# First stage of a hybrid decoder step planned anew: loads on the sync queue beside the page gathers, TensorE's order pinned, three dense tiles in step

## The chip, the cores and the metric

The kernel runs on one core of a Trainium2 chip. The metric is the time of one execution on the device in microseconds (us); lower is better. The engines are PE (TensorE, matrix products), DVE (VectorE), ACT (ScalarE), POOL (GpSimd) and SP (the sync engine, which only issues DMAs here). Each engine works through its instructions in the order in which they are written to it and waits for the semaphores of others.

## The reference

The program is one step of a single-layer hybrid decoder for 520 tokens: 512 of a prompt and one for each of 8 samples. What matters here is its beginning:

```python
def _layer(x, c, pos, conv_buf, h0, ffn_buf, nsa_fn, p):
    mod = jnp.einsum("bd,de->be", jax.nn.silu(c), p["ada_w"]) + p["ada_b"]
    sh1, sc1, g1, sh2, sc2, g2 = jnp.split(mod[:, None, :], 6, axis=-1)
    h = _rmsnorm(x, p["norm1_w"]) * (1.0 + sc1) + sh1
    proj = h @ p["w_in"]
    z, xbc, dt_raw, q, kv, att_g, merge_g = jnp.split(proj, ...)
    # then: causal conv and SSD scan of xbc, attention with a paged cache, merge, ConvFFN

def _compress(k, pe, w1, w2):      # on the rows of the pages, among others
    part = jnp.einsum("bjshd,sde->bjhe", sub, w1[r * CMP_STRIDE:(r + 1) * CMP_STRIDE])
    return jnp.einsum("bnhe,ed->bnhd", jax.nn.silu(hid + part), w2)

past = cache_nsa_kv[page_table]    # the pages of the samples, gathered by a table
```

## The kernel before, in words

Tokens (520) lie along the free axis and features on the 128 partitions. The function `phase_a` is the first stage. It has five kinds of work:

- **Pages.** 16 gathers (`gather`, an indirect DMA on POOL's queue, 128 x 512 numbers, 262 KB each) bring the pages into the tiles S_13 and KS. `compress_s` multiplies them with the weights w1k and w1v (tile `w1`, four loads of 512 KB). It runs in four parts of 32 rows in the order of instructions (each a fp32 product which the trace shows as two records, so 64 records), each part with four gathers. Afterwards ACT and DVE add the two halves (`ch`, `chs`), and a DMA stores them (`dr_hs`).
- **Modulation.** Eight tiles `ada`, nb = 0 to 7, each with two loads of 512 KB and eight narrow products with the conditioning vector (`sc`, from cT); ACT copies the result to `adas`, TensorE transposes it twice ("flip"), DVE reduces it to `mod`. Tiles nb and nb + 4 together give the shift and scale for the rows h(2 nb) and h(2 nb + 1).
- **Norm.** x comes in four loads of 532 KB. ACT squares it, DVE adds the eight squares, TensorE sums over partitions (`sums`), DVE forms 1/rms (`rstd5`), TensorE spreads it over the partitions (`spread`), and ACT copies it into `rs`.
- **h.** `h(k)`, k = 0 to 7: x times rs, scaling and shift, and a split into a high part `h_hi` (ACT) and a low part `h_lo` (DVE, x minus h_hi).
- **The first dense tiles.** A weight tile (1024 x 128) is split into a high part `wh` (ACT, line 308) and a low part `wl` (line 310, DVE and POOL in turns) in two halves of 512 columns. A dense tile is, for each k, hi x hi, hi x lo and lo x hi on two token halves: 8 x 6 = 48 matmuls. Before, misc and B are computed in step in `phase_a`; C and then the convolution tiles x0 to x3 and z follow outside.

A planner runs through the program once and fixes the order on each engine by its own model of times; an instruction named in `behind` is held behind another in that order without a semaphore. `queue` (line 399) loads on SP, `queue_pool` (line 403) on POOL. Of these, before, SP carries w1, cT and const, then the stores of `dr_hs` and the last modulation weights; POOL carries the gathers, x and the first modulation and w_in weights. PSUM has two wide tiles `d` (dense results, pages) and four narrow ones `s`. A conv tile's result leaves its wide tile through ACT and DVE. `Weights` loads, splits and frees the weight tiles; it has six raw buffers here.

## Time and profile before

| | |
|---|---|
| Median of 3 runs | 1470.51 us (1470.27 to 1474.33) |
| Profiled execution, its own time | 1468.96 us |
| Its span in the trace | 1467.1 us |
| Mean granted TensorE clock | 0.983 |
| PE busy | 1404.2 us (96%) |
| DVE busy | 942.2 us (64%) |
| ACT busy | 697.6 us (48%) |
| POOL busy | 473.7 us (32%) |

The trace has the span of one execution, a little less than its time. Busy times are sums over the span; a stage is read from its own rows.

### The profile page before, as it was taken

The page shows a single profiled execution, that of the slowest core. Times are in us where ns is not written, and L with a number is a line of the kernel's source. Part 1 is how long each engine was busy: PE and PEld are TensorE (multiplying, and loading weights), DVE is VectorE, ACT ScalarE, POOL GpSimd, SP SyncE. Part 2 cuts the span into 40 slices and gives each one's busy share as a digit, 9 for nine tenths or more (in the row PEclk, how much of TensorE's full clock was granted, in tenths as well). Part 3 has the DMA queues.
Part 4 walks back from the last instruction along what each step waited for, and adds up shares of the span by engine and source line. Part 5 has one row for each costly group of instructions (what it writes and reads, how often), then busy time and mean ns, then how long its engine had stood idle before and what let it go on. Part 6 is the DMA issues. An engine that isn't in the chain of part 4 may idle for free.

```text
span 1467.1 us, 28899 instructions
## 1 busy us (share of the span) xinstructions
PE 1404.2 (96%) x11403; PEld 1283.1 (87%) x11403; DVE 942.2 (64%) x1851; ACT 697.6 (48%) x1540; POOL 473.7 (32%) x488
## 2 busy tenths in 40 slices
PE   7899899999999899999999999999999999999996
PEld 6689789998898798887878877899889999999996
DVE  1768899788879856858667562134586636653663
ACT  2346657565664424646556463233554324432443
POOL 6213564463565754312213011122421111111113
PEclk9989999999999999999999999999999999999998
DMA  8734546345354384314122124525423233433221
GB/s 301 296 97 159 176 136 213 112 143 199 122 170 143 117 278 159 110 39 130 59 94 81 44 101 150 182 84 210 164 72 98 82 110 130 137 112 98 80 77 59
DMA packets 73799, 195.30 MB, mean 133 GB/s; under 512 B 8480, under 2 KB 21312, under 8 KB 73408
## 3 DMA queue, kind: packets, MB, share of 16 engines
q1 hardware_dynamic: 67968, 175.05, 36.2%
q0 software_dynamic: 5152, 17.86, 3.4%
q8 instruction: 90, 1.47, 0.4%
q10 hardware_dynamic: 544, 0.54, 0.1%
q14 instruction: 45, 0.37, 0.1%
HBM read 173.10 MB, written 24.49 MB: 135 GB/s over the span
## 4 chain that ended last, share of the span: by engine, by line
PE 69%; DVE 10%; DMA 8%; ACT 4%; issue 4%; POOL 4%; SPq 0%; DVEq 0%; POOLq 0%; ACTq 0%
PE d L385 54%; PE s L385 13%; DMA wr<-w_in 3%; DVE st L417 2%; PE s L1370 2%; DVE S L414 1%; DMA st<-sst 1%; DVE wl L310 1%; DMA P<-pool_kv,idx 1%; DMA csx<-dr_cs 1%; ACT wh L308 1%; ACT E L430 1%; ACT S L430 1%; DVE E L414 1%; POOL wl L310 1%
## 5 line engine op out<-in xcount | busy, mean ns | idle before, releaser
L385 PE MATMUL d<-S,wh 128*128 128x256 f32 (+1 forms) x4640 | 834.9, 291 | 27.2 <-DVE S L414 9.4
L385 PEld LDWEIGHTS d<-S,wh 128*128 128x128 f32 x4640 | 670.8, 191 | 57.7 <-issue 27.3
L385 PE MATMUL d<-S,wl 128*128 128x256 f32 (+1 forms) x2672 | 557.6, 287 | 0.2 <-DVE wl L310 0.2
L385 PEld LDWEIGHTS d<-S,wl 128*128 128x128 f32 x2672 | 423.2, 190 | 5.7 <-issue 4.7
L308 ACT ACTIVATE wh<-wr 128x512 fp32r<-128x512 f32 (+1 forms) x354 | 217.3, 623 | 388.9 <-PE d L385 302.5
L310 POOL TENSOR_TENSOR wl<-wr,wh 128x512 fp32r<-128x512 f32 (+1 forms) x153 | 205.9, 1347 | 607.6 <-ACT wh L308 581.8
L310 DVE TENSOR_TENSOR wl<-wr,wh 128x512 fp32r<-128x512 f32 (+1 forms) x201 | 154.6, 769 | 119.4 <-ACT wh L308 106.0
L385 PE MATMUL d<-M,wh 128*128 128x256 f32 (+1 forms) x960 | 197.0, 284 | 2.4 <-DVE M L417 1.7
L385 PEld LDWEIGHTS d<-M,wh 128*128 128x128 f32 x960 | 149.7, 188 | 3.0 <-DVE M L417 1.9
L430 ACT ACTIVATE P<-s,sm 128x256 f32<-128x256 f32 (+3 forms) x128 | 66.7, 524 | 64.5 <-DVE sm L1352 60.4
L414 DVE TENSOR_TENSOR S<-S,S 128x520 f32<-128x520 f32 (+3 forms) x86 | 65.8, 770 | 31.8 <-ACT S L430 28.7
L1352 DVE TENSOR_REDUCE sm<-s 128x1 f32<-128x512 f32 (+3 forms) x96 | 57.1, 596 | 32.0 <-PE s L385 31.2
L430 ACT ACTIVATE S<-S 128x520 f32<-128x520 f32 (+4 forms) x87 | 49.7, 581 | 49.4 <-DVE S L414 20.8
L417 DVE SCALAR_TENSOR_TENSOR S<-d,fww,S 128x511 f32<-128x511 f32 x84 | 62.9, 749 | 12.0 <-ACT S L430 12.0
L430 ACT ACTIVATE PT<-s 128x512 f32<-128x512 f32 (+2 forms) x96 | 49.9, 523 | 39.9 <-PE s L1370 39.5
L385 PE MATMUL s<-PT,V 128*64 128x128 f32 x640 | 64.3, 286 | 0.0
L417 DVE SCALAR_TENSOR_TENSOR st<-st,dts,so 128x128 f32<-128x128 f32 x128 | 60.0, 517 | 6.4 <-ACT so L430 4.3
L385 PE MATMUL s<-K,Q 128*128 128x256 f32 (+3 forms) x256 | 60.1, 336 | 1.7 <-ACT PT L430 1.6
L422 DVE TENSOR_SCALAR P<-P,sm,gates 128x256 f32<-128x256 f32 (+3 forms) x128 | 58.9, 480 | 2.4
L430 ACT ACTIVATE so<-bcb,xd 128x128 f32<-128x128 f32 x128 | 41.0, 391 | 34.9 <-DVE ys L1060 21.2
L417 DVE SCALAR_TENSOR_TENSOR S<-d,cwh,S 128x511 f32<-128x511 f32 (+2 forms) x72 | 53.4, 742 | 2.4 <-ACT S L430 2.0
L1370 PE MATMUL s<-cst,P 128*128 128x128 f32 x320 | 52.3, 276 | 0.8 <-DVE P L422 0.7
(312 smaller groups left out, 1686.7 us busy)
## 6 DMA issues: line engine op xcount, KB each, us to landing
wr<-w_in SPq DMA_DIRECT2D x75, 512.0 KB, 3.6
wr<-w_up SPq DMA_DIRECT2D x44, 512.0 KB, 3.8
wr<-ada SPq DMA_DIRECT2D x36, 512.0 KB, 4.2
st<-sst SPq DMA_DIRECT2D x32, 256.0 KB, 2.9
csb<-dr_cs SPq DMA_DIRECT2D x16, 512.0 KB, 4.2
o_ssms<-st SPq DMA_DIRECT2D x32, 256.0 KB, 2.1
wr<-w_so SPq DMA_DIRECT2D x16, 512.0 KB, 3.5
wr<-w_dn SPq DMA_DIRECT2D x16, 512.0 KB, 3.4
```

The lines of the kernel that those rows point to most:

```text
L308: self.nc.scalar.activation(hi[:, :n], raw[:, k0:k1], AF.Copy)
L310: eng.tensor_tensor(out=lo[:, :n], in0=raw[:, k0:k1], in1=hi[:, :n], op=ALU.subtract)
L385: r = self.nc.tensor.matmul(out, lhsT=l, rhs=r, start=start, stop=stop)
L414: return (eng or self.nc.vector).tensor_tensor(out=out, in0=a, in1=b, op=op)
L417: return self.nc.vector.scalar_tensor_tensor(out=out, in0=a, scalar=s, in1=b, op0=op0, op1=op1)
L422: return (eng or self.nc.vector).tensor_scalar(out=out, in0=a, scalar1=s1, scalar2=s2, op0=op0, op1=op1)
L430: return self.nc.scalar.activation(out, a, func, scale=scale, **kw)
L1352: nc.vector.tensor_reduce(sm[:, 0], ps, AX.X, ALU.max, negate=True)
L1370: nc.tensor.transpose(ps[:, i * n + k * P:i * n + (k + 1) * P], pr[:, i, k * P:(k + 1) * P], self.ident)
```

## The change

The diff, cut to its core:

```diff
-WARM = 12
+WARM = 10
+FILL = 18
@@ Weights.prepare
-            self.nc.scalar.activation(hi[:, :n], raw[:, k0:k1], AF.Copy)
+            r = self.nc.scalar.activation(hi[:, :n], raw[:, k0:k1], AF.Copy)
+            if self.hold:
+                self.hold(r)
+                self.hold = None
@@ Emit.mm
+        if self.pin is not None:
+            self.behind(r, self.pin)
+            self.pin = None
@@ Emit.dense
+        if apart:
+            d = [self.ps_s()[:, 0:n] for _, _, n in HALVES]
@@ phase_a
+            for i in range(16):
+                g = self.gather(KS[i // 8][:, i % 8].rearrange("p j i c -> p (j i c)"), A["pool_cmp"], i)
+                self.last_pool = self.behind(g, self.last_pool)
+            W = Weights(nc, pa, self.jobs(), self.order and self.order[0], raws=RAW0, parts=PART0,
+                        queue=lambda i: self.queue, first=[first[i // 4][:, i % 4] for i in range(8)])
+            self.queue(cT, A["cT"])
+            W.load(2)
             for j, nm in enumerate(("w1k", "w1v")):
                 for half in range(2):
                     self.queue(w1[:, j, half], A[nm][half])
-                if j == 0:
-                    self.queue(cT, A["cT"])
             self.queue(self.cst[:, :CONST_EARLY], A["const"][:, :CONST_EARLY])
-            def load_x(k):
-                self.queue_pool(x[:, k:k + 2], A["xT"][:, k:k + 2])
...
+            W.load(4)
+            for k in range(0, KD, 2):
+                self.queue(x[:, k:k + 2], A["xT"][:, k:k + 2])
             W.load()
+            self.W.load()
...
             def h(k):
+                self.tt(x[:, k, :], x[:, k, :], r, ALU.mult, nc.gpsimd if k % 2 else nc.vector)
...
+            products(a[0])
+            pin()
+            self.fill(FILL)
+            pages()
+            products(a[4])
+            flips(a[0])
+            pages()
...
+            products(a[1], a[5])
+            flips(a[4])
+            pages()
+            flips(a[1], a[5])
+            pin()
+            self.sums(d, sq, True, True)
+            rb = self.rstd5(d, DM, pa)
+            products(a[2], a[6])
+            self.W.hold = W.hold = lambda r: self.behind(r, self.last_ada)
...
+            flips(a[2], a[6])
+            for k in range(4):
+                h(k)
+            pages()
+            products(a[3], a[7])
+            names = [("C", 0), ("misc", 0), ("B", 0)]
+            tiles = [self.in_tile(n, None if i == 0 else W, i == 0) for i, n in enumerate(names)]
+            for k in range(KD + 1):
+                if k < 2:
+                    h(4 + k)
+                elif k == 2:
+                    flips(a[3], a[7])
+                    h(6)
+                    h(7)
+                for n, g in zip(names, tiles):
+                    try:
+                        next(g)
+                    except StopIteration as e:
+                        self.early[n] = e.value
+            c = self.t(cp, "S2", [P, T], 4)
+            for (_, t0, n), p in zip(HALVES, self.early["C", 0]):
+                self.act(c[:, t0:t0 + n], p)
@@ compress_s
-            nc.sync.dma_start(self.dr_hs[j], hs.rearrange("p x n -> p (x n)"))
+            nc.scalar.dma_start(self.dr_hs[j], hs.rearrange("p x n -> p (x n)"))
```

`pin` holds the next matmul behind the one written before it. `fill` issues bf16 matmuls on a tile of zeros whose result nobody reads. `apart` puts the halves of C's result into two narrow PSUM tiles, from which ACT copies them; `tokens` (not shown) lets the conv tile read either kind of result.

On SP, the head of the program before. w_11 is the tile of w1, cT the conditioning, wr a weight tile, chs the sums of the pages:

```order
L1156 DMA page_88<-page 128x16
L399 DMA w_11_94<-w1k 128x1024 x2
L399 DMA cT_95<-cT 128x256
L399 DMA w_11_94<-w1v 128x1024 x2
L399 DMA cst_63<-const 128x184
L1188 DMA dr_hs_153<-chs_326 128x512
L399 DMA wr_448<-ada 128x1024
L399 DMA wr_496<-ada 128x1024
L1188 DMA dr_hs_153<-chs_332 128x512
```

And the same place of the changed kernel (S_15 and S_16 hold the modulation weights of tiles 0, 4 and 1, 5, S_7 is x):

```order
L1210 DMA page_86<-page 128x16
L408 DMA cT_93<-cT 128x256
L408 DMA S_15_112<-ada 128x1024 x2
L408 DMA w_11_92<-w1k 128x1024 x2
L408 DMA w_11_92<-w1v 128x1024 x2
L408 DMA cst_63<-const 128x184
L408 DMA S_15_112<-ada 128x1024 x2
L408 DMA S_7_85<-xT 128x1040 x4
L408 DMA S_16_113<-ada 128x1024 x4
L408 DMA wr_132<-ada 128x1024
```

The weights of the modulation and x have come to SP's queue, in the order in which TensorE uses them, and the stores of dr_hs have left it; further weights follow without a store between them.

On PE, behind the warm matmuls, before. d_154 and d_155 are the results of the pages, s_351 to s_410 those of modulation tiles 0, 4, 1, 5, and the rows of L595 are flips:

```order
L385 MATMUL d_154<-S_13_102,w_11_94 128x4x4x8 x16
L385 MATMUL d_155<-S_13_102,w_11_94 128x4x4x8 x16
L385 MATMUL d_154<-KS_103,w_11_94 128x4x4x8 x16
L385 MATMUL d_155<-KS_103,w_11_94 128x4x4x8 x16
L385 MATMUL s_252<-ones_64,S_24_253 128x1 x5
L385 MATMUL d_154<-KS_103,w_11_94 128x4x4x8 x16
L385 MATMUL d_155<-KS_103,w_11_94 128x4x4x8 x16
L385 MATMUL s_338<-cst_63,rstdb_291 128x128 x2
L385 MATMUL s_342<-cst_63,rstdb_291 128x128 x2
L385 MATMUL s_342<-cst_63,rstdb_291 128x8
L385 MATMUL s_351<-S_15_124,sc_149 32x256 x8
L385 MATMUL s_360<-S_15_124,sc_149 32x256 x8
```

And of the changed kernel, behind ada0 and the 18 fillers (d_187 and d_188 are the pages, s_221 is ada4, s_293 and s_304 are ada1 and ada5, s_269 the sums):

```order
L391 MATMUL d_187<-S_13_94,w_11_92 128x4x4x8 x16
L391 MATMUL d_188<-S_13_94,w_11_92 128x4x4x8 x16
L391 MATMUL s_221<-S_15_112,sc_151 32x256 x8
L614 MATMUL s_232<-cst_63,adas_165 128x128 x2
L391 MATMUL d_187<-S_13_94,w_11_92 128x4x4x8 x16
L391 MATMUL d_188<-S_13_94,w_11_92 128x4x4x8 x16
L391 MATMUL s_293<-S_16_113,sc_151 32x256 x8
L391 MATMUL s_304<-S_16_113,sc_151 32x256 x8
L614 MATMUL s_315<-cst_63,adas_230 128x128 x2
L391 MATMUL d_187<-KS_95,w_11_92 128x4x4x8 x16
L391 MATMUL d_188<-KS_95,w_11_92 128x4x4x8 x16
L391 MATMUL s_269<-ones_64,S_31_270 128x1 x5
```

The modulation tiles stand between the parts of the pages now instead of behind them; ada2 and ada6 with 12 of the last part's 32 rows follow, then the spread, the other 20 rows, ada3 and ada7, and then the dense tiles.

On POOL, behind the gathers, before (identb and negtri are constants, wl the low halves of weights):

```order
L573 CAST identb_672<-cst_63 128x128
L310 TENSOR_TENSOR wl_1_445<-wr_134,wh_1_444 128x512
L310 TENSOR_TENSOR wl_1_493<-wr_136,wh_1_492 128x512
L575 CAST negtri_674<-cst_63 128x256
L310 TENSOR_TENSOR wl_1_782<-wr_676,wh_1_781 128x512
L310 TENSOR_TENSOR wl_1_851<-wr_678,wh_1_850 128x512
L422 TENSOR_SCALAR gates_760<-gates_760 128x240
```

And of the changed kernel:

```order
L592 CAST identb_760<-cst_63 128x128
L423 TENSOR_TENSOR S_7_85<-S_7_85,rs_155 128x520 x4
L594 CAST negtri_762<-cst_63 128x256
L315 TENSOR_TENSOR wl_1_565<-wr_401,wh_1_564 128x512
L315 TENSOR_TENSOR wl_1_671<-wr_407,wh_1_670 128x512
L315 TENSOR_TENSOR wl_1_659<-wr_144,wh_1_658 128x512
L315 TENSOR_TENSOR wl_1_872<-wr_146,wh_1_871 128x512
```

Four of the eight products x times rs (S_7 with rs) have come to POOL, ahead of all splits of weights; the first two splits of before (misc and B) stood ahead of rs and stand behind it now.

## Rows read from the trace of the kernel before

**Rows 1.** The head of the page: busy times of the engines, and the chain of work that ended last, by engine.

```profile
PE 1404.2 (96%) x11403; PEld 1283.1 (87%) x11403; DVE 942.2 (64%) x1851; ACT 697.6 (48%) x1540; POOL 473.7 (32%) x488
...
PE 69%; DVE 10%; DMA 8%; ACT 4%; issue 4%; POOL 4%; SPq 0%; DVEq 0%; POOLq 0%; ACTq 0%
```

**Rows 2.** The table of stretches of the core: from:to in us, its length, busy us of PE, PEld, DVE, ACT and POOL (with the number of instructions), then the mean granted clock of PE, the busy share of the DMA engines and the GB/s that they moved.

```profile
12.80:47.60 34.80, 34.80 (x308) 33.92 (x308) 8.62 (x17) 7.54 (x14) 20.28 (x31) 0.94 0.93 343
47.60:58.10 10.50, 7.16 (x78) 3.42 (x75) 9.42 (x32) 4.34 (x11) 1.17 (x1) 0.84 0.68 224
58.10:91.85 33.75, 28.25 (x190) 24.78 (x189) 24.29 (x64) 15.04 (x33) 5.29 (x5) 0.80 0.38 142
150.00:250.00 100.00, 92.10 (x722) 84.40 (x721) 92.80 (x163) 67.29 (x172) 56.19 (x59) 0.97 0.54 170
```

**Rows 3.** The timeline of PE from 0 to 100 us: start, busy us, line, operation and tiles, number, and in brackets the idle time before it and what ended it. The rows are, in this order, the warm matmuls, two page parts together and one alone, the sums, the spread, a pair of modulation tiles, a flip, the first dense matmuls behind a wait, C's first with its wait, and six matmuls further of C at full clock, from the start of one row to that of the next, which is x0's first.

```profile
1.39 5.30 PE L385 MATMUL s<-warm 128*128 128x512 bf16 x12 [1.39 <-POOL warm L653]
12.80 16.64 PE L385 MATMUL d<-S,w 128*128 128x128 f32 x128 [6.11 <-DMA S<-pool_cmp,idx]
29.28 7.31 PE L385 MATMUL d<-KS,w 128*128 128x128 f32 x64
36.43 1.17 PE L385 MATMUL s<-ones,S 128*128 128x1 f32 x10
...
44.69 1.18 PE L385 MATMUL s<-cst,rstdb 128*128 128x128 f32 x10
45.80 1.93 PE L385 MATMUL s<-S,sc 128*32 128x256 f32 x32
...
51.99 0.44 PE L595 MATMUL s<-cst,adas 128*128 128x128 f32 x2
...
74.49 0.51 PE L385 MATMUL d<-S,wh 128*128 128x256 f32 x2 [1.68 <-ACT S L430]
...
82.74 1.24 PE L385 MATMUL d<-S,wh 128*128 128x256 f32 x4 [1.66 <-ACT Z L430]
...
91.12 0.64 PE L385 MATMUL d<-S,wh 128*128 128x256 f32 x4
...
91.84 0.64 PE L385 MATMUL d<-S,wh 128*128 128x256 f32 x4
```

**Rows 4.** The DMA of the windows 5 to 7, 7 to 9, 9 to 11 and 35 to 38 us (packets, MB and mean GB/s of the window, for the first and the last; the queue, its packets, MB and the share of the 16 engines' time, for the first three, one row each; q1 is SP's queue, q0 POOL's); the issue of the first gather on POOL (start, us); and the time from issue to landing of the 16 gathers.

```profile
DMA packets 328, 0.81 MB, mean 404 GB/s; under 512 B 35, under 2 KB 163, under 8 KB 328
q1 hardware_dynamic: 328, 0.81, 102.3%
...
q0 software_dynamic: 15, 0.06, 7.5%
...
q0 software_dynamic: 202, 0.69, 84.7%
...
DMA packets 351, 1.27 MB, mean 422 GB/s; under 512 B 42, under 2 KB 42, under 8 KB 351
...
4.34 1.16 POOL L1163 DMA_INDIRECT S<-pool_cmp,idx  x1 [2.35 <-DVE idx L417]
...
DMA to landing us min/median/max: 3.4/3.9/6.2
```

**Rows 5.** The table of stretches, as above, where the granted clock (the number ahead of the DMA share) changes.

```profile
17.00:17.50 0.50, 0.50 (x5) 0.50 (x5) 0.00 (x0) 0.00 (x0) 0.41 (x1) 0.76 1.07 416
...
76.00:88.00 12.00, 10.06 (x46) 9.66 (x46) 6.97 (x21) 3.13 (x6) 0.70 (x1) 0.50 0.00 0
...
89.00:90.00 1.00, 1.00 (x10) 1.00 (x10) 0.01 (x1) 0.99 (x2) 0.00 (x0) 1.00 0.03 0
```

**Rows 6.** The timelines of DVE and, behind the last line of dots, of POOL: the splits of weights (wl<-wr,wh), x times rs (S<-S,rs), scalings (S<-S,a,mod), and subtractions for h_lo (S<-S,S).

```profile
47.80 1.51 DVE L310 TENSOR_TENSOR wl<-wr,wh 128x512 fp32r<-128x512 f32 x1
49.24 4.96 DVE L414 TENSOR_TENSOR S<-S,rs 128x520 f32<-128x520 f32 x8
...
60.56 2.52 DVE L414 TENSOR_TENSOR S<-S,S 128x520 fp32r<-128x520 f32 x4
...
66.45 3.49 DVE L414 TENSOR_TENSOR S<-S,S 128x520 fp32r<-128x520 f32 x2
69.86 0.68 DVE L310 TENSOR_TENSOR wl<-wr,wh 128x512 fp32r<-128x512 f32 x1
...
75.18 0.55 DVE L422 TENSOR_SCALAR S<-S,a,mod 128x512 f32<-128x512 f32 x1 [0.16 <-ACT S L430]
75.64 1.30 DVE L414 TENSOR_TENSOR S<-S,S 128x520 fp32r<-128x520 f32 x2
...
47.51 1.27 POOL L310 TENSOR_TENSOR wl<-wr,wh 128x512 fp32r<-128x512 f32 x1 [0.23 <-ACT wh L308]
...
66.39 2.99 POOL L310 TENSOR_TENSOR wl<-wr,wh 128x512 fp32r<-128x512 f32 x2 [3.05 <-ACT wh L308]
```

**Rows 7.** The timelines of ACT (a table load, the first step of a conv tile, and Z, the copy of misc's result) and, behind the last line of dots, of SP's queue (the first store of dr_hs).

```profile
75.36 1.28 ACT L430 ACT_TABLE_LOAD   x1
...
81.33 0.78 ACT L430 ACTIVATE S<-d,cbh,cwh 128x520 f32<-128x520 f32 x1 [4.45 <-DVE convo L859]
82.01 0.68 ACT L430 ACTIVATE Z<-d,cst 96x520 f32<-96x520 f32 x1
...
47.91 0.33 SPq L1188 DMA_DIRECT2D dr_hs<-chs  x1
```

More of the change, by code (lines that the diff above doesn't have):

```diff
@@ L273, in place, with load @@
         return self.pool, (self.raws if key[0] == "r" else self.parts) - (more or 0)
-    def load(self):
-        while self.loaded < len(self.order):
+    def load(self, upto=None):
+        while self.loaded < (len(self.order) if upto is None else min(upto, len(self.order))):
             i, m = self.loaded, len(self.first)
@@ L499, in dense @@
             for j, (a, b) in enumerate(((0, 0), (0, 1), (1, 0))):
-                for c0, t0, n in HALVES:
-                    m = self.mm(d[:, c0:c0 + n], l[a], r[b][:, t0:t0 + n], start=(k == 0 and j == 0),
+                for out, (c0, t0, n) in zip(o, HALVES):
+                    m = self.mm(out, l[a], r[b][:, t0:t0 + n], start=(k == 0 and j == 0),
                                 stop=(k == nk - 1 and j == 2))
@@ L554, in in_tile, with tokens @@
         w = (W or self.W).get(name)
-        d = yield from self.dense(w, KD, lambda k: self.h_hi[:, k, :], lambda k: self.h_lo[:, k, :], W=W)
+        d = yield from self.dense(w, KD, lambda k: self.h_hi[:, k, :], lambda k: self.h_lo[:, k, :], W=W, apart=apart)
         return d
+    @staticmethod
+    def tokens(d):
+        return d if d.shape[-1] == T else d[:, OFF:OFF + T]
     def setup(self):
@@ L650, in warm, with fill @@
     def warm(self, pool):
-        z = self.t(pool, "warm", [P, 512], dt=BF16)
-        self.nc.gpsimd.memset(z, 0.0)
+        self.z = self.t(pool, "warm", [P, 512], dt=BF16)
+        self.nc.gpsimd.memset(self.z, 0.0)
+        self.fill(WARM)
+    def fill(self, n):
         d = self.ps_s()
-        for _ in range(WARM):
-            self.mm(d, z[:, 0:P], z)
+        for _ in range(n):
+            self.mm(d, self.z[:, 0:P], self.z)
     def phase_a(self):
@@ L694, in phase_a, with pin, products, flips @@
             self.preload(AF.Sqrt)
[L695 to L717 removed]
+            self.h_hi = self.h_lo = None
+            r = self.t(pa, "rs", [P, T])
+            def pin():
+                self.pin = self.last_mm
+            def products(*gens):
+                for g in gens:
+                    for _ in range(3):
+                        pin()
+                        next(g)
+            def flips(*gens):
+                for g in gens:
+                    pin()
+                    next(g)
+                    self.pin = None
+            def pages():
+                pin()
+                next(comp)
             def h(k):
+                self.tt(x[:, k, :], x[:, k, :], r, ALU.mult, nc.gpsimd if k % 2 else nc.vector)
                 a1 = self.t(pa, "a1", [P, 16], 4)
@@ L748, in phase_a @@
-            for n, g in zip(names, tiles):
-                try:
-                    next(g)
-                except StopIteration as e:
-                    self.early[n] = e.value
+            comp = self.compress_s(KS, w1, pa)
+            a = {nb: self.ada(nb, W, pa) for nb in range(8)}
+            products(a[0])
+            pin()
+            self.fill(FILL)
[3 more added lines that the diff above has]
+            pages()
+            d = self.ps_s()
+            sq = self.t(cp, "S2", [P, T], 4)
@@ new lines, in phase_a @@
+            self.behind(self.act(sq, x[:, 0, :], AF.Square), self.last_ada)
+            for k in range(1, KD):
+                s = self.t(cp, "S2", [P, T], 4)
+                self.act(s, x[:, k, :], AF.Square)
+                self.tt(sq, sq, s, ALU.add)
+            products(a[1], a[5])
+            flips(a[4])
+            pages()
+            flips(a[1], a[5])
+            pin()
+            self.sums(d, sq, True, True)
+            rb = self.rstd5(d, DM, pa)
+            self.h_hi = self.t(cp, "S16", [P, KD, T], 4, F32R)
@@ new lines, in phase_a @@
+            self.h_lo = self.t(cp, "S16", [P, KD, T], 4, F32R)
+            products(a[2], a[6])
+            self.W.hold = W.hold = lambda r: self.behind(r, self.last_ada)
+            pin()
+            for part in range(2):
+                lo, hi = self.span(part)
+                cs = self.PARTS[part]
+                self.act(r[:, lo:hi], self.spread(rb[:, cs[0]:cs[-1] + 1], part))
+            flips(a[2], a[6])
[3 more added lines that the diff above has]
+            products(a[3], a[7])
@@ new lines, in phase_a @@
+            for _ in comp:
+                pass
+            pin()
+            names = [("C", 0), ("misc", 0), ("B", 0)]
[9 more added lines that the diff above has]
+                    try:
+                        next(g)
+                    except StopIteration as e:
+                        self.early[n] = e.value
```

82 lines of the change are left out of this document (20 added, 62 removed).

## The prediction

> **What bounds the kernel now.** I read the head of the page first [rows 1]: TensorE is busy in 96% of the span, and it and its two helpers fill the chain that ended last. So a gain can only come from a stretch in which TensorE waits or runs at half clock. The table of stretches [rows 2] shows where that is: from 12.8 to 47.6 us it is busy throughout, but it misses 3.34 us from 47.6 to 58.1 and 5.50 us from 58.1 to 91.85, where the granted clock is also only 0.80, and its timeline shows 7.50 us before the first page part (1.39 and 6.11) [rows 3]. On every engine the order of the two kernels is the same behind the first fifth to quarter of its instructions, so all that the change can do is to shift the instant at which the convolution tiles x0, x1, ... run, and everything behind them, as a block. In the kernel before, x0 starts at 91.84 us [rows 3], right behind the last matmul of C.
>
> TensorE's rows [rows 3] give the prices: a page part (64 records) 7.3 us, a pair of modulation tiles 1.93 us, a flip 0.44 us, the sums 1.17 us, the spread 1.18 us, and six dense matmuls 0.72 us at full clock, so 0.12 us each.
>
> The DMA rows [rows 4] say what can arrive: 404 to 422 GB/s when the engines are full, so about 0.41 MB/us, counted from 3.5 us on. Gathers have 262 KB each.
>
> **The change part by part.**
>
> *Loads on the sync queue.* The order shows ada0 ahead of the w1 tiles, then ada4, x, ada1, ada5. Ahead of the first page part stand 0.13 + 1.05 + 2.10 MB there and four gathers, 1.05 MB: 4.33 MB / 0.41 = 10.6 us, plus 3.5, plus 0.8 to land = 14.9. The ten warm matmuls, ada0 and the 18 fillers (18 x 0.44 = 7.9 us, 0.44 from 5.30 / 12) end at about the same time. I take 15.0, against 12.80 before. What is lost there comes partly back, because ada0 is then done and because before the pages ran at half clock until 17.25 [rows 5].
>
> Pages 1, ada4, a flip, pages 2: 15.0 + 7.3 + 0.97 + 0.44 + 7.3 = 31.0. Then ada1 and ada5 wait for their weights: 8.65 MB on the sync queue (0.13 + 1.05 + 2.10 + 0.09 + 1.05 + 2.13 + 2.10) and all 4.19 MB of gathers make 12.84 MB / 0.41 = 31.3, plus 4.3 = 35.6. At the 343 GB/s that the stretch from 12.8 to 47.6 really moved [rows 2] it is 41.7; that is the other bound. I take 35.6, because the windows in which a queue was full are the nearest rows, and the changed queue has no waits in it.
>
> *TensorE's pinned order.* From 36.1: the rest of ada5 0.35, pages 3 7.3, flips 0.8, sums 1.17, ada2 and ada6 1.93, 12 of 32 matmuls of pages 4 2.7, spread 1.18: 51.5, and the copies of 1/rms (rs) are there at 52.0. Before, rs was there at 49.2 (x times rs starts at 49.24 [rows 6]). So this stage starts 2.8 us later, with more of TensorE's work already done: flips 2 and 6, the rest of pages 4 (4.6) and ada3, ada7 (1.93) are all that stands between rs and the dense tiles, and end at 59.
>
> *From rs to the last h_lo.* This term decides. Before, it took 27.8 us, from 49.15 to 76.94 (its last row starts at 75.64 and takes 1.30 [rows 6]). Four of the eight multiplications x*rs move from VectorE (0.62 us each, 4.96 / 8 [rows 6]) to GpSimd; the rows have none there, but the split of a weight is the same operation on 512 instead of 520 columns: 1.28 us. The bounds are that they run beside VectorE (cost nothing) or in turns with it. The rows point to turns: at 66.45 two subtractions that otherwise take 0.63 us each (2.52 / 4) took 3.49 us while GpSimd ran two splits in 2.99 us, which alone take 2 x 1.28; a split on VectorE at 47.80 took 1.51 instead of 0.68 us while GpSimd's ran from 47.51 to 48.78. So I add up both engines as one: x*rs 4 x 0.62 + 4 x 1.30 = 7.7; remaining reductions of modulation tiles and small operations 4.5; eight scalings 4.4 (0.55 each); eight subtractions 5.0; the two additions behind the pages 1.6; weight splits 4 x 0.68 + 4 x 1.28 = 7.8, of which before one of each was done before rs. Together 31.0, so the last h_lo is ready at 83.0 (before 76.94).
>
> The Trainium skill, page "SBUF — State Buffer", section "SBUF: two separate sides", speaks against moving work to GpSimd for this reason: it has the two engines share one pair of ports under an exclusive lock, so that a VectorE operation with two inputs in SBUF and a GpSimd operation that reads SBUF block one another completely. The trace agrees (3.49 us where 1.26 would do). By that rule the term is 31.0 us, without it 20.7.
>
> *Three tiles in step.* C, misc and B have 3 x 48 = 144 matmuls, 17.3 us. The first low half of a weight is ready at about 69.7: the first 15.8 us of the list above, plus some 2 us in which ScalarE, in program order, puts small copies that wait for VectorE ahead of the weights' high halves. From there 17.3 us give 87.0; the last h_lo gives 83.0 plus two steps of the three tiles (36 matmuls, 4.3 us) = 87.3. TensorE waits from 59 to about 69, and after the wait of 1.68 us before 74.49 the clock stood at half until 89 [rows 3, 5]; here at most a few waiting matmuls meet the low clock, 1.3 us. So the three tiles end at 88.6. Before, misc and B ended at 81.1 (82.74 less C's wait of 1.66) and C at 91.84 [rows 3]. The in-step order gives TensorE 18 instead of 12 matmuls for each step of h (2.2 us against 1.4), so I count no further waits between steps.
>
> *What then waits.* misc and B hold both wide PSUM buffers, so x0 waits for ScalarE: the conv 0.78, a table load 1.28, Z 0.68 [rows 7], 2.75 us together. The kernel before has the same wait for Z ahead of C. x0 starts at 91.35, against 91.84.
>
> *Costless parts.* C's copies out of PSUM (about 0.55 us on ScalarE) lie under x0. The dr_hs stores on ScalarE's queue take 0.33 us of issue [rows 7] in a stage where ScalarE is idle half the time; before, the first of them held the sync queue until 47.91. That wait is gone, which the sum has in it: ada3 and ada7 now wait only for TensorE.
>
> The sum is -0.5 us on the profiled execution's 1468.96: 1468.5. The runs' median lies 1.55 us above that execution, so I forecast 1470.0 for the median.
>
> **Rivals.** A time within 4.4 us (0.3%) can't be told from no change here.
>
> *A, faster.* GpSimd's operations run beside VectorE's. For it: most of VectorE's scalings read only one tile, and not every pair in the trace collides. Against it: the two rows above. The last h_lo is then at 72.7, the first low half at 62.8, the tiles end between 62.8 + 17.3 = 80.1 and 84.5, and x0 starts between 82.9 and 87.3: 4.6 to 9.0 us gained. VectorE is busy 92.8% from 150 to 250 us [rows 2], which may take some back. About 1463. TensorE's work alone forbids more.
>
> *B, slower: gathers behind the sync queue.* From 5 to 7 us the sync queue had all of the engines (102.3%) though a gather had been issued at 4.34; from 7 to 9 the gathers had 7.5%; they moved when the sync queue ran dry, 84.7% from 9 to 11 [rows 4]. Before that cost 3 us at most (landing 3.4 to 6.2). Now the sync queue is full for some 30 us. If the gathers get a share s of 0.41 MB/us, the first four land at 8.3 + 1.05 / (0.41 s) + 0.8: 14.2 at a half, 16.8 at a third, 21.9 at a fifth, 34.7 at a tenth. Each us beyond 15 delays the pages, and all behind them, unless the wait for ada5 hides it: that wait is 5 us long, and the pages' later gathers use it up too. By these terms it decides below a quarter: at a fifth about 1475, at a tenth about 1487.
>
> The Trainium skill, page "DMA: Bandwidth & Descriptors", section "Queues, rings and completion order", has each DMA engine take turns between the queues that have work, packet by packet. By that the gathers would keep a share near a third and B would not happen; the 0% and 7.5% here fit it badly.
>
> *D, slower: the loads come no sooner.* The DMA engines were busy 93% from 12.8 to 47.6 already [rows 2], at 343 GB/s. If the new mix moves no more than that, ada5 is there at 41.7, and rs, h and x0 come up to 6 us later: 1476. Against it: 422 GB/s from 35 to 38 [rows 4].
>
> **How the numbers follow.** My forecast (within 0.3%) 0.41, its own range 1466 to 1474 (1.3 us of clock, 2 us at ScalarE, some overlap on GpSimd). A 0.32. B 0.16, D 0.11: slower 0.27. To leave out no more than 2 in 10, the range reaches from 1462 (A's middle and a little) to 1477 (D, and B down to a fifth).
>
> **What would show it.** The pages' first matmul at 15 to 16.5 us; if it is beyond 20, B. ada5 at 36; at 41 or later, D. Multiplications of 1.3 us on GpSimd with VectorE's operations next to them stretched to about 2 us: the turns; unstretched: A. The last h_lo at 83, x0 at 91.4. The prediction is wrong if x0 starts before 87 or after 96, or if later tiles do not shift with x0.

## The result, and the profile after

The changed kernel takes 1486.72 us (median of 4 runs, 1485.95 to 1487.09) against 1471.0 us of the kernel before (4 runs, 1470.27 to 1474.33) on the same chip: slower by 15.7 us, ratio 1.0102 with the interval 1.0084 to 1.0119. The forecast was 1470.0, with a range from 1462 to 1477. Two executions of later kernels were slow, one of v_adafirst (5431 us) and one of v_adafirst2 (3724 us), and are in no median.

The head of the page after, as [rows 1]: busy time of each engine, and the chain that ended last.

```profile
PE 1411.1 (95%) x11419; PEld 1288.5 (87%) x11419; DVE 948.6 (64%) x1847; ACT 698.4 (47%) x1542; POOL 475.1 (32%) x474
...
PE 73%; DVE 11%; DMA 7%; ACT 3%; issue 3%; POOL 2%; SPq 0%; DVEq 0%; ACTq 0%; POOLq 0%
```

TensorE is busy 6.9 us longer than before with 16 matmuls more; the span grew by 17.1 us (1484.2 against 1467.1). The head doesn't say where. TensorE's timeline does; these rows answer to [rows 3] (start, busy us, line, operation and tiles, number, idle time before it and what ended it).

```profile
8.34 4.06 PE L391 MATMUL s<-warm 128*128 128x512 bf16 x18
...
14.72 7.38 PE L391 MATMUL d<-S,w 128*128 128x128 f32 x64 [2.32 <-DMA S<-pool_cmp,idx]
...
37.50 0.64 PE L391 MATMUL s<-S,sc 128*32 128x256 f32 x8 [0.51 <-DMA S<-ada]
...
68.55 0.80 PE L391 MATMUL d<-S,wl 128*128 128x256 f32 x2 [2.50 <-DVE wl L315]
...
88.62 0.40 PE L391 MATMUL d<-S,wl 128*128 128x256 f32 x2
91.44 0.99 PE L391 MATMUL d<-S,wh 128*128 128x256 f32 x4 [2.43 <-ACT Z L439]
...
109.36 1.21 PE L391 MATMUL d<-S,wh 128*128 128x256 f32 x4 [4.13 <-DVE S L426]
...
143.88 1.02 PE L391 MATMUL s<-xdd,bt 128*128 128x512 f32 x2
```

In order: the 18 fillers, the first page part, the last quarter of ada5, the first low half of a dense weight, the end of the three tiles, x0, x2, and the first matmul of the scan's state (`s<-xdd,bt`). Up to x0 they stand where the forecast put them (14.7 for 15.0, 37.5 for 36.1, 68.6 for 69.7, 89.0 for 88.6, 91.44 for 91.35). x0 starts 0.40 us earlier than in the kernel before. But x2 waits 4.13 us, and the state matmul, which before stood at

```profile
137.78 1.02 PE L385 MATMUL s<-xdd,bt 128*128 128x512 f32 x2
```

comes 6.1 us later. The loss arises behind the point at which I stopped reading, and it grows on the way. Three later rows show where: two further matmuls of the state, and behind them a row of VectorE from which on all engines have the same order again. Before:

```profile
242.25 1.02 PE L385 MATMUL s<-xdd,bt 128*128 128x512 f32 x2
...
293.65 1.02 PE L385 MATMUL s<-xdd,bt 128*128 128x512 f32 x2
...
328.79 1.13 DVE L417 SCALAR_TENSOR_TENSOR st<-st,dts,so 128x128 f32<-128x128 f32 x4
```

After:

```profile
249.14 1.02 PE L391 MATMUL s<-xdd,bt 128*128 128x512 f32 x2
...
307.40 1.02 PE L391 MATMUL s<-xdd,bt 128*128 128x512 f32 x2
...
342.73 1.14 DVE L426 SCALAR_TENSOR_TENSOR st<-st,dts,so 128x128 f32<-128x128 f32 x4
```

The shift is 6.1 us at the first state matmul, then 6.9, 13.8 and 13.9: about 7 us arise in one stretch of the scan, from the first to the third of these rows, which takes 93.6 us instead of 86.5. The last 3.2 of the 17.1 us arise behind it.

Two questions follow: why x0 in time doesn't give the scan in time, and why 6 us become 16.

**From the end of misc and B to the scan.** The table of stretches, columns as in [rows 2], from the end of misc and B to the first state matmul, of the kernel before:

```profile
81.10:91.84 10.74, 9.10 (x53) 9.10 (x54) 8.07 (x23) 4.73 (x8) 1.83 (x2) 0.64 0.01 2
91.84:118.30 26.46, 26.46 (x215) 25.30 (x214) 18.44 (x41) 18.12 (x42) 4.43 (x6) 1.00 0.49 142
118.30:137.80 19.50, 18.83 (x159) 18.58 (x158) 17.15 (x30) 11.44 (x27) 10.45 (x11) 1.00 0.49 163
sum 56.70, PE 54.39 PEld 52.98 DVE 43.65 ACT 34.29 POOL 16.71; mean PE 18.13 PEld 17.66 DVE 14.55 ACT 11.43 POOL 5.57
```

The kernel after, from its end of misc and B (89.0):

```profile
89.00:91.44 2.44, 0.02 (x1) 0.00 (x0) 1.16 (x5) 2.38 (x4) 0.00 (x0) 1.00 0.38 114
91.44:109.36 17.92, 13.79 (x101) 13.61 (x102) 15.93 (x35) 7.25 (x13) 3.52 (x3) 0.89 0.13 39
109.36:125.25 15.89, 15.89 (x116) 14.92 (x117) 9.99 (x23) 9.46 (x23) 2.50 (x3) 0.91 0.50 140
125.25:143.90 18.65, 18.65 (x159) 18.61 (x158) 16.48 (x25) 13.40 (x35) 11.17 (x12) 1.00 0.56 175
sum 54.90, PE 48.34 PEld 47.13 DVE 43.55 ACT 32.50 POOL 17.19; mean PE 12.09 PEld 11.78 DVE 10.89 ACT 8.12 POOL 4.30
```

VectorE has the same work between the two marks, 43.65 and 43.55 us: the conv of B and C, misc's dt chain, the convs of x0 to x3, the weight splits. Before, 8.07 us of it were done in the first stretch, while TensorE ran C alone. With C in step all three tiles end at 89.0, misc and B 7.9 us later than before, and none of that work can start sooner. x0 finds it in its way: VectorE, just ahead of x2's wait,

```profile
104.16 0.75 DVE L426 SCALAR_TENSOR_TENSOR S<-d,cwh,S 128x511 f32<-128x511 f32 x1
...
105.94 1.14 DVE L862 RECIPROCAL S<-S 128x160 f32<-128x160 f32 x1
107.00 0.64 DVE L426 SCALAR_TENSOR_TENSOR S<-d,cwh,S 128x510 f32<-128x510 f32 x1
...
108.48 0.73 DVE L426 SCALAR_TENSOR_TENSOR S<-d,cwh,S 128x509 f32<-128x509 f32 x1
```

and ScalarE:

```profile
101.81 1.28 ACT L439 ACT_TABLE_LOAD   x1
...
103.35 0.77 ACT L439 ACTIVATE S<-d,cbh,cwh 128x520 f32<-128x520 f32 x1
```

x0's conv (on VectorE the three steps that read `d`) is mixed with the dt chain (L862), and its first step on ScalarE stands behind that chain's table load. Its last step frees x0's wide PSUM buffer, for which x2 waits, only at 109.2 (108.48 + 0.73).

**Behind the scan's start.** ScalarE of the kernel after at 268 us, and TensorE's wait there:

```profile
268.75 0.63 ACT L439 ACTIVATE sq<-yd 128x512 f32<-128x512 f32 x1 [2.16 <-DVE yd L423]
269.29 0.61 ACT L310 ACTIVATE wh<-wr 128x512 fp32r<-128x512 f32 x1
272.23 0.63 ACT L439 ACTIVATE csx<-csx 128x512 f32<-128x512 f32 x1 [2.32 <-DMA csx<-dr_cs]
272.76 0.59 ACT L439 ACTIVATE S<-d 128x520 f32<-128x520 f32 x1
```

```profile
273.40 1.24 PE L391 MATMUL d<-S,wh 128*128 128x256 f32 x4 [3.15 <-ACT S L439]
274.44 0.64 PE L391 MATMUL d<-S,wl 128*128 128x256 f32 x2
```

The same place in the kernel before:

```profile
259.88 0.64 ACT L430 ACTIVATE sq<-yd 128x512 f32<-128x512 f32 x1 [2.41 <-DVE yd L414]
260.41 0.62 ACT L308 ACTIVATE wh<-wr 128x512 fp32r<-128x512 f32 x1
260.94 0.58 ACT L430 ACTIVATE S<-d 128x520 f32<-128x520 f32 x1
261.42 0.27 ACT L430 ACTIVATE bt<-s 128x128 f32<-128x128 f32 x1
262.68 0.63 ACT L430 ACTIVATE csx<-csx 128x512 f32<-128x512 f32 x1 [0.99 <-DMA csx<-dr_cs]
```

It is another order: the exponential of csx, which waits for a transfer, now stands ahead of the copy `S<-d` that frees a PSUM buffer. TensorE waits 3.15 us and comes back at half clock (granted 0.50 from 273.4 to 278.5 us; two low-half matmuls take 0.64 us instead of 0.40). This wait lies between 249.14 and 307.40. Compared record by record, the two traces run the scan in different orders up to 289 us of the kernel before on TensorE, 318 on ScalarE and 324 on VectorE; behind that the orders are the same.

### The profile page after: what moved, and what is told of

The parts are those of the page before. It is cut to its first block, busy times and chain, and to the rows that moved or that the text cites. A ratio compares the mean times of both kernels' runs of the same rounds, so it can differ in the third digit from the quotient of the medians.

```text
span 1484.2 us, 28939 instructions
## 1 busy us (share of the span) xinstructions
PE 1411.1 (95%) x11419; PEld 1288.5 (87%) x11419; DVE 948.6 (64%) x1847; ACT 698.4 (47%) x1542; POOL 475.1 (32%) x474
## 4 chain that ended last, share of the span: by engine, by line
PE 73%; DVE 11%; DMA 7%; ACT 3%; issue 3%; POOL 2%; SPq 0%; DVEq 0%; ACTq 0%; POOLq 0%
PE d L391 57%; PE s L391 13%; PE s L1424 2%; DVE st L426 2%; DMA S<-ada 2%; DVE S L423 2%; DMA wr<-w_in 1%; DMA csb<-dr_cs 1%; DVE wl L315 1%; ACT E L439 1%; DVE E L423 1%; DMA wr<-ada 1%; DVE S L426 1%; ACT wh L310 1%; ACT so L439 1%
## 5 line engine op out<-in xcount | busy, mean ns | idle before, releaser
L315 POOL TENSOR_TENSOR wl<-wr,wh 128x512 fp32r<-128x512 f32 (+1 forms) x153 | 210.3, 1376 | 635.3 <-ACT wh L310 575.9
L315 DVE TENSOR_TENSOR wl<-wr,wh 128x512 fp32r<-128x512 f32 (+1 forms) x201 | 150.9, 751 | 118.4 <-ACT wh L310 106.4
L423 DVE TENSOR_TENSOR S<-S,S 128x520 f32<-128x520 f32 (+3 forms) x86 | 64.9, 758 | 17.1 <-ACT S L439 12.6
```

Of the source, the lines that this page charges most:

```text
L315: eng.tensor_tensor(out=lo[:, :n], in0=raw[:, k0:k1], in1=hi[:, :n], op=ALU.subtract)
L423: return (eng or self.nc.vector).tensor_tensor(out=out, in0=a, in1=b, op=op)
```

## The experiments

Marks of each profiled execution sum up what follows: the end of misc and B, x0's start, the first state matmul with its shift against 137.8, and "stretch", the time between the two later marks (242.25 to 328.79 in the kernel before). Then the difference of the medians of kernel and before of the same set of runs; "rest" is that difference less the shift. A mark is of one execution: the same code run again on another chip gave the state matmul 0.1 us (v_fused) and 2.7 us (v_adafirst) apart, and a_ord1, whose code up to there is that of after, has it 3.1 us later. So a rest is known to about 3 us.

| kernel | misc and B end | x0 | state matmul | shift | stretch | median, difference | rest | ratio, interval |
|---|---|---|---|---|---|---|---|---|
| before | 81.1 | 91.84 | 137.8 | | 86.5 | | | |
| after | 89.0 | 91.44 | 143.9 | +6.1 | 93.6 | +15.7 | +9.6 | 1.0102 (1.0084 to 1.0119) |
| a_two | 86.2 | 94.17 | 139.3 | +1.5 | 86.9 | +1.8 | +0.3 | 1.0011 (0.9996 to 1.0026) |
| a_mult | 89.4 | 91.81 | 146.1 | +8.3 | 91.7 | +17.5 | +9.2 | 1.0140 (1.0101 to 1.0178) |
| a_both | 83.7 | 91.68 | 136.8 | -1.0 | 86.1 | +0.8 | +1.8 | 1.0012 (0.9997 to 1.0027) |
| a_fill1 | 89.9 | 92.28 | 145.4 | +7.6 | 93.8 | +15.8 | +8.2 | 1.0103 (1.0074 to 1.0132) |
| b_delay | 80.8 | 96.70 | 142.7 | +4.9 | 88.3 | +5.2 | +0.3 | 1.0030 (1.0010 to 1.0050) |
| a_noc | 89.2 | 91.59 | 139.5 | +1.7 | 92.5 | +9.9 | +8.2 | 1.0064 (1.0041 to 1.0086) |
| b_three | 85.7 | 88.62 | 141.9 | +4.1 | 88.9 | +11.9 | +7.8 | 1.0084 (1.0060 to 1.0109) |
| b_hs | 79.3 | 87.31 | 136.4 | -1.4 | 86.6 | +0.8 | +2.2 | 1.0008 (0.9995 to 1.0021) |
| a_ord1 | 90.8 | 93.27 | 147.0 | +9.2 | 89.6 | +12.4 | +3.2 | 1.0092 (1.0070 to 1.0115) |
| a_ord2 | 88.7 | 91.15 | 143.7 | +5.9 | 89.4 | +11.2 | +5.3 | 1.0080 (1.0062 to 1.0098) |
| v_clate | 91.3 | 93.72 | 145.9 | +8.1 | 90.9 | +14.4 | +6.3 | 1.0099 (1.0077 to 1.0121) |
| v_adafirst | 86.2 | 94.14 | 139.3 | +1.5 | 86.9 | +2.2 | +0.7 | 1.0017 (1.0003 to 1.0030) |
| v_adafirst2 | 87.7 | 95.66 | 141.9 | +4.1 | 86.0 | -0.7 | -4.8 | 0.9998 (0.9983 to 1.0013) |
| v_fused | 84.4 | 92.41 | 137.5 | -0.3 | 86.9 | +0.4 | +0.7 | 1.0000 (0.9989 to 1.0011) |
| v_fused2 | 84.3 | 92.28 | 137.4 | -0.4 | 87.0 | -1.1 | -0.7 | 0.9996 (0.9983 to 1.0009) |

**C out of step (a_two).** The kernel after, with misc and B in step and C behind them, as before:

```
-            names = [("C", 0), ("misc", 0), ("B", 0)]
-            tiles = [self.in_tile(n, None if i == 0 else W, i == 0) for i, n in enumerate(names)]
+            names = [("misc", 0), ("B", 0)]
+            tiles = [self.in_tile(n, W) for n in names]
...
```

> The changed kernel with C taken out of the step: misc and B alone run over k, C follows as a tile of its own, as before. Theory 1 (the loss lies behind x0: with three results ready at once, the convs of B and C and the dt chain of misc have no TensorE work of C left to hide under): the wait of 4.1 us ahead of x2 goes, x0 starts at 92 to 95, the first state matmul (s<-xdd,bt) comes back from 143.9 to 137 to 140, and the time is 1470 to 1477. Theory 2 (VectorE and GpSimd in turns ahead of x0 are the cause): C's 5.8 us are only moved, 1484 to 1488.

The time is 1473.57, before 1471.75: of 15.7 us, 1.8 are left, within the interval of nothing. x0 starts 2.7 us *later* than in the kernel after, and the kernel is some 14 us faster: x0's start is not what decides. The whole loss hangs on C in step. Its way to the scan is not only the later end of misc and B, though: they end 5.1 us later than before here too, and the state matmul comes only 1.5 us later. From after to a_two the state matmul gains 4.6 us, 2.8 by the earlier end and 1.8 behind it.

**All multiplications on VectorE (a_mult), and both edits (a_both).**

```
-                self.tt(x[:, k, :], x[:, k, :], r, ALU.mult, nc.gpsimd if k % 2 else nc.vector)
+                self.tt(x[:, k, :], x[:, k, :], r, ALU.mult)
```

> The changed kernel with all eight multiplications x*rs on VectorE. Theory 1: the last h_lo and x0 come up to 2.7 us earlier (four times 1.3 us against four times 0.62 in turns), the rest stays: 1483 to 1487. Theory 2: the stage between rs and the last h_lo shortens by more than 4 us and the time falls to 1481 or below. If GpSimd's operations ran beside VectorE's after all, it gets slower by 1 to 3 us.

> Both edits together, so what is left of the change is the loads on the sync queue, the fillers, the pinned order and the stores on ScalarE's queue. Theory 1: as with C alone taken out, less at most 2.7 us: 1468 to 1476. Theory 2: as with the multiplications on VectorE alone. Theory 3 (loads, fillers and pins are themselves the loss): 1483 or more.

a_mult gained nothing: 1489.25 lies above the ranges expected if GpSimd and VectorE work in turns. The outcome expected if they work side by side, 1 to 3 us slower, fits the time but not the stage, which got shorter. From the first multiplication x*rs to the last h_lo it takes 27.9 us, after 28.9: the turns with GpSimd cost 1 us, and the time doesn't show it. a_both takes 26.5 and ends level with before (1472.53): new loads, pinned order, fillers and the stores on ScalarE's queue are together worth nothing that can be measured. a_mult and a_both differ by C in step alone, as after and a_two do: 16.7 us between their medians, 9.3 at the state matmul.

**One filler instead of 18 (a_fill1).**

> The changed kernel with one filler matmul instead of 18. All theories: the first page part waits for its gather at 14.7 anyway, so 1485 to 1488; if the fillers do what keeps TensorE's clock up, the pages begin at half clock and the time grows by 1 to 4 us, unless the wait for ada1 and ada5 behind pages 2 takes that up. It also shows whether the order of the later stages, which this edit leaves as it is, gives the same time again.

The first page part then begins at the lower clock (granted 0.50 up to 19 us, in after 1.00 from its start):

```profile
15.13 9.31 PE L391 MATMUL d<-S,w 128*128 128x128 f32 x64 [6.32 <-DMA S<-pool_cmp,idx]
```

9.31 us instead of 7.38, but the wait for ada5's weights takes all but 0.6 us of it up (page part 3 starts at 38.96 for 38.34), and the time is that of after (1487.53). The fillers buy nothing here. Nor do they always hold the clock: in a_mult, with all 18, the granted clock was 0.66 from 15.04 to 17 us and 0.50 from 17 to 19, and the first page part took 9.01 us.

**A delay and nothing else (b_delay).** The kernel before, with 28 more matmuls between C and x0, whose result nothing reads; apart from a few rows ahead of 130 us the order is unchanged.

> The kernel before with 28 extra matmuls of 512 columns (about 6.2 us, on a result that nobody reads) between C and x0; the order of all other instructions stays as it was except for a few rows. Theory 1a (a delay ahead of x0 is carried through to the end as it is; what made 6 us in front of the scan into 15 at the end is the other order of instructions up to 290 us): 1475 to 1479, shift of the scan's first state matmul 5 to 7 us and the same at 300 and 900 us. Theory 1b (a delay there grows by itself, as loads and engines then meet differently): 1483 or more.

```profile
90.33 6.53 PE L386 MATMUL s<-S 128*128 128x512 f32 x28
```

x0 and the scan come 4.9 us later, the median 5.2 us (6 runs, 1470.66 to 1483.07; the interval of the ratio is 1.5 to 7.4 us). So by the medians a delay of x0 is carried to the end about one to one, as the forecast had it. The profiled execution, the slowest of the six, does not say so:

```profile
249.44 1.02 PE L386 MATMUL s<-xdd,bt 128*128 128x512 f32 x2
...
302.16 1.02 PE L386 MATMUL s<-xdd,bt 128*128 128x512 f32 x2
...
337.73 1.13 DVE L421 SCALAR_TENSOR_TENSOR st<-st,dts,so 128x128 f32<-128x128 f32 x4
```

These rows are 7.2, 8.5 and 8.9 us late, and its span is 14.1 us longer than that of the kernel before (1481.2 against 1467.1). The same shift at 300 us, as expected, did not come in it. What holds in it too is that a delay in the old order leaves the stretch between these rows nearly as it was, 88.3 us for 86.5, where the kernel after needs 93.6. Behind the stretch the profiled executions of all these kernels gain or lose between -1.0 and 5.7 us against that of the kernel before, which was itself 2.0 us under its median; the 3.2 us of after lie in that spread.

**Less work for VectorE (a_noc).** The kernel after without the three multiply-adds of C's conv in the first group, 2.2 us of VectorE's work; that part of the convolution is left out.

> The changed kernel without the three multiply-adds of the conv of tile C of group 0 (2.2 us on VectorE; that part of the computation is left out). Its order stays that of the changed kernel. Theory 1a: the wait of 4.1 us ahead of x2 shrinks by about 2 us, the rest of the loss stays: 1482 to 1486. Theory 1c (C's conv is the whole trouble): x2 does not wait and the time is 1478 or less.

```profile
106.24 0.72 PE L391 MATMUL d<-S,wh 128*128 128x256 f32 x4 [0.88 <-DVE S L426]
```

x2's wait falls from 4.13 to 0.88 us, the state matmul comes 4.4 us sooner, and of the 15.7 us 9.9 are left (1480.76, just under the expected range): VectorE between misc and the scan is the bound there. The rest (8.2 us) stays, and so does the long stretch (92.5).

**C in step in the kernel before (b_three).** First stage, loads and engines of before, only C in step with misc and B (and its weights loaded first).

> The kernel before with one thing of the change: C in step with misc and B. Loads, TensorE's order, the multiplications on VectorE and the stores of dr_hs stay as they were. Theory 1: the same loss as of the whole change, 1482 to 1492, with a wait of 4 to 6 us ahead of x2. Rival: it costs only where the pages end late, then 1468 to 1476.

```profile
106.50 1.21 PE L391 MATMUL d<-S,wh 128*128 128x256 f32 x4 [5.64 <-DVE S L426]
```

x0 starts 3.2 us sooner than in the kernel before, x2 then waits 5.64 us, and the time is 11.9 us longer, 7.8 of it behind the scan's start. This is most of the loss of the change without the rest of the change. In its profiled execution, whose span is 13.6 us longer than that of the kernel before, only 2.4 us lie in the stretch (88.9); 5.7 lie behind it, where the order is that of before.

**The dr_hs stores alone (b_hs).** `nc.sync.dma_start` becomes `nc.scalar.dma_start` in the kernel before.

> The kernel before with the two stores of dr_hs issued from ScalarE's queue. The loads of ada3 and ada7 no longer stand behind them on the sync queue. If their weights were what the first stage waited for, x0 comes 1 to 3 us earlier: 1468 to 1470. If they wait for free buffers anyway, no change: 1469 to 1473.

x0 starts 4.5 us sooner, the state matmul 1.4, and the time doesn't move (1471.64 against 1470.85). Once more x0's start does not decide: between x0 and the scan TensorE waits for VectorE four times by more than 0.4 us, 3.0 us in all.

**Another order in the scan (a_ord1, a_ord2).** The kernel after; the exponential of csx in group 1, chunk 3, is emitted behind the copy for z that it held up, and one step is given 500 or 1500 more in the planner's units, which moves its choice.

```
...
             if c:
-                self.act(ex[c], ex[c], AF.Exp)
+                if (g, c) != (1, 3):
+                    self.act(ex[c], ex[c], AF.Exp)
...
+            if (g, c) == (1, 3):
+                yield 500.0
...
+                if (g, c) == (1, 3):
+                    self.behind(self.act(e, e, AF.Exp), self.zw)
```

> The changed kernel with nothing else than another order in the scan of the first two groups: an exponential of the scan (csx, group 1, fourth chunk) is held behind the copy of a z tile, and the scan yields to the dense tiles a little earlier there, so ScalarE copies a finished tile out of PSUM before it waits for csx's load. Work, loads and order up to about 235 us stay. Theory 1a (a part of the loss is the order that came about behind the first stage): up to 230 us the same shift as the changed kernel (about 7 us against before), then no wait of 3 us of TensorE at 270 and 3 to 7 us less at the end: 1479 to 1484. Theory 1b (the delay itself grows, whatever the order): 1485 to 1488.

> The same with the scan yielding somewhat later: a second order of the same work. Theory 1a: 1479 to 1484 again, or another time than the first, since the order decides. Theory 1b: 1485 to 1488, as the first.

TensorE's 3.15 us are gone in both, and the stretch falls from 93.6 us to 89.6 and 89.4. The five other kernels with C in step have the order of after in that stretch and take 88.9 (b_three) to 93.8 us; the nine with the old order there take 86.0 to 88.3 (b_delay). So by these executions the order costs some 2 to 7 us in this stretch, 7 in the kernel after, and another order of the same work has 4 of them back; b_three and b_delay lie so close that the size is soft. The medians agree roughly: the rest is 6.3 to 9.6 us in the kernels with the order of after, and 3.2 and 5.3 in these two, of which a_ord1, at 1484.75, is just above its expected range. The two edits move the exponential and the planner's choice together, so their shares are not known.

**C's conv later (v_clate).** The kernel after with the conv of C written behind that of x1.

> The changed kernel with the conv of tile C, whose result already lies in SBUF, written behind x1 instead of ahead of x0. Nothing is left out. If C's conv, in VectorE's order ahead of x0's, is what x2 waits for, that wait shrinks from 4.1 to about 1 us and the first state matmul comes 3 to 5 us earlier; the order behind it stays of the changed kernel's kind, so the time is 1479 to 1484. If the dt chain of misc is what holds x0's buffer, the wait stays above 3 us and the time is 1484 to 1488.

x2's wait is gone, yet from the end of misc to the state matmul it takes 54.6 us (after 54.9), and the time is 14.4 us above before. TensorE now waits for VectorE at four other places ahead of the scan (0.92, 1.15, 0.66 and 1.56 us). The wait of x2 was where the backlog showed, not the loss itself: VectorE has the same work to do wherever C stands in it. Neither of the two expected outcomes came: the wait went, and the time did not.

**Modulation weights ahead of x (v_adafirst, repeated as v_adafirst2).** a_both with `W.load(8)` instead of `W.load(4)`.

> C alone after misc and B, all multiplications on VectorE, and on the sync queue the weights of ada1 and ada5 ahead of x. TensorE waited from 33.9 to 38.1 us for these weights; they now land about 5 us earlier, and x, which is needed 8 us later, in their place. Page part 3 starts at 33 to 35 instead of 38.3, rs, h and x0 come 3 to 4 us earlier: 1467 to 1470, against 1472.5 with x first. Rival: the sums now wait for the squares of x, and nothing is gained: 1471 to 1474.

> The kernel of v_adafirst once more, since the profiled executions of that call, v_clate's too, whose first stage is that of the changed kernel, show TensorE held for 7 us in the first page part by nothing that the trace names. If that belongs to those executions, page part 1 takes 7.4 us here, rs is there at 49 to 51, x0 starts 3 to 4 us earlier than in the kernel before, and the time is 3 to 4 us below it. If it belongs to the queue's order, it shows again and the time is that of before or 1 to 3 us above.

The waits for ada5 are gone, but the first page part takes 14.7 instead of 7.4 us (from 14 to 30 us TensorE is busy 11.44 us, at a granted clock of 0.79), with holes that nothing in the trace explains:

```profile
23.22 0.27 PE L391 MATMUL d<-S,w 128*128 128x128 f32 x1 [0.35 <-issue]
25.33 0.39 PE L391 MATMUL d<-S,w 128*128 128x128 f32 x2 [1.83 <-issue]
```

No gain, where 3 to 4 us were hoped for: 1.0017 and 0.9998. With 7 us lost to holes in the profiled executions, these runs don't show what the order of the loads alone is worth.

**Fewer VectorE operations for h (v_fused, repeated as v_fused2).** v_adafirst with the product x*a*rs in one instruction and the subtraction for h_lo taking the shift in.

```
...
+                self.stt(v, v, a1[:, 0:1], r[:, 0:SEQ], ALU.mult, ALU.mult)
+                self.act(self.h_hi[:, k, 0:SEQ], v, AF.Identity, bias=sh[:, 0:1])
...
+                self.stt(self.h_lo[:, k, 0:SEQ], v, sh[:, 0:1], self.h_hi[:, k, 0:SEQ], ALU.add, ALU.subtract)
...
```

> As before, and h without the separate scaling: x*rs and the scale in one operation of VectorE with two multiplications, shift and subtraction in another, so two operations of about 0.72 us for each k instead of three of 0.62, 0.55 and 0.63. The last h_lo comes another 1.5 to 3 us earlier: 1465 to 1469. Rival: ScalarE, which waits for the first of them, sets the pace: no gain over the run before.

> The kernel of v_fused once more, for the same reason. Without the hold in page part 1: the last h_lo at 74 to 77, and 3 to 7 us below the kernel before. With it: the time of before again.

From the first product with rs to the last h_lo it takes 25.0 us instead of 26.5 (a_both), and the times are 1.0000 and 0.9996 of before. The first page part, with the same holes, takes 15.4 and 15.5 us, and the last h_lo comes at 81.5 and 81.4, not at 74 to 77. No version beat the kernel before by what can be measured.

## Why the prediction was wrong

**Right, step by step up to x0.** *Loads on the sync queue*: first page part at 14.72 for 15.0, the last quarter of ada5 at 37.50 for 36.1. *From rs to the last h_lo*: 28.9 us, from the first multiplication at 53.7 to the end of the last subtraction at 82.6, where 31.0 were added up and 83.0 came out. The end is so close partly by luck: the stage began 1.7 us later than counted and was 2.1 us shorter. The sum also goes from 35.6 to 36.1 without a reason. *Three tiles in step* ended at 89.0 for 88.6, and *what then waits* was ScalarE's Z, x0 at 91.44 for 91.35. One term was off without harm: the 18 fillers took 4.06 us, where 7.9 were counted from the warm matmuls, and TensorE waited 2.32 us for the gather behind them.

**Rival B fell.** DMA queues of the kernel after from 8 to 12 us (q1 is the sync queue, q0 the gathers; packets, MB, share of the 16 engines' time):

```profile
q1 hardware_dynamic: 272, 0.99, 61.5%
q0 software_dynamic: 192, 0.66, 40.6%
```

From 16 to 20 us it is 52.9% and 49.7%. The gathers had 40 to 50% beside a full sync queue, far above the quarter below which they would have held the pages up. The Trainium skill, page "DMA: Bandwidth & Descriptors", section "Queues, rings and completion order", has the engines take turns between queues with work; these shares agree with it, better than the 7.5% in [rows 4] did. **Rival D fell**: 411 to 417 GB/s in those windows, where 343 was its premise. **Rival A** fell too: it had the last h_lo at 72.7.

**The step that failed** is in the first paragraph of the prediction: "all that the change can do is to shift the instant at which the convolution tiles x0, x1, ... run, and everything behind them, as a block". It has two errors.

*x0's start was the wrong mark.* With C behind misc and B in the new first stage (a_two, a_both, v_adafirst, v_fused and the repeats), the scan starts 45.1 to 46.3 us after x0 and 53.1 to 54.3 after the end of misc and B, with TensorE busy for 51.3 to 51.6 of these us; b_delay too has 46.0 after x0. There a later x0 does mean a later scan. With C in step (after, a_mult, a_fill1, b_three, a_ord1, a_ord2, v_clate) it is 52.2 to 54.3 us after x0 and 54.6 to 56.7 after the end of misc and B; TensorE is busy for only 47.5 to 49.7 of them, and its waits behind x0 are for VectorE, which has 41.8 to 44.4 us of work there. a_noc, with less of that work, needs 50.3. The kernel before stood close to both (46.0 after x0, 56.7 after misc and B), and so b_hs, with x0 4.5 us sooner, gained only 1.4. The forecast had the end of misc and B in its own sum, 81.1 before and 88.6 after, and made nothing of the 7.5 us between them. *Costless parts* counted C's copies under x0, but not the work of B, C and misc that had run under C's dense matmuls and lost its cover. a_noc, a_two and b_three show it. This is 6.1 of the 15.7 us. Each piece of that work had a row in the trace of before; their sum over that stretch would have told. The prediction's own last sign of being wrong, later tiles that do not shift with x0, is what came.

*The order is not the same behind the first quarter.* By instruction count that was right: 1132 of ScalarE's 1542 records in the new trace, 1392 of VectorE's 1847 and 9320 of TensorE's 11419 form one tail that is unchanged from before. But in time this tail starts at 318, 324 and 289 us of the kernel before, and the scan's part ahead of it, from 138 us on, was planned anew. I named that share as if it ended at x0, and took the differing part for the edited stage. In the profiled execution this cost 7.0 us in the stretch from 249.14 to 342.73, and a_ord1 and a_ord2 have about 4 of them back by another order of the same work. Another 0.8 us arise between the scan's start and that stretch and 3.2 behind it, where the order is the old one again; what these and the other 3 us of the stretch are made of is open.

The rivals of the slower side had 0.27 between them, for mechanisms that did not occur; the right time was outside the range, because no slower case in it looked behind x0.

## What to carry to other kernels

When work of the bottleneck engine is moved, ask not only when its next tile starts but what the other engines used to do under the moved work: sum their busy time from the release of that work to the next point that needs it, and compare it with the gap that is left. Where a planner sets the order, look at where in *time* the two orders join again and price what lies ahead of that point as open in both directions. A part of the change that ends on schedule by one mark can still be late by another, so follow at least two marks, one for each engine that has a backlog.

## What the runs showed of the hardware

VectorE and GpSimd do hold each other up, also on tiny operations. VectorE of the kernel after:

```profile
54.52 1.59 DVE L423 TENSOR_TENSOR S<-S,rs 128x520 f32<-128x520 f32 x1
...
57.24 3.56 DVE L423 TENSOR_TENSOR S<-S,rs 128x520 f32<-128x520 f32 x2
...
68.42 1.25 DVE L423 TENSOR_TENSOR S<-S,mod 128x8 f32<-128x8 f32 x1
```

GpSimd beside it:

```profile
53.70 6.54 POOL L423 TENSOR_TENSOR S<-S,rs 128x520 f32<-128x520 f32 x4 [29.55 <-ACT rs L439]
...
65.36 8.30 POOL L315 TENSOR_TENSOR wl<-wr,wh 128x512 fp32r<-128x512 f32 x4 [4.31 <-ACT wh L310]
```

An addition of eight columns took 1.25 us, otherwise 0.15, and multiplications that take 0.62 us alone [rows 6] took 1.59 and 1.78. The Trainium skill, page "SBUF — State Buffer", section "SBUF: two separate sides", states the lock between the two that the prediction counted with, and the rows agree. Yet taking those four multiplications off GpSimd made the stage only 1.0 us shorter (a_mult), since VectorE then does them itself.

TensorE's holes marked "issue" in the first page part came in every profiled execution of the last two sets of runs (those of v_clate to v_fused2), also in v_clate with the first stage of after, and in none of those before. Some 7 us of the page part were lost to them and to the lower clock around them (granted 0.79 from 14 to 30 us in v_adafirst). What holds TensorE there was not found, and whether the executions without a profile had them isn't known.
